# Gated delta rule recurrence: gate loads at a chunk's tail, merged outputs stored by chunk, one step between an inverse's loads and its products

## The chip, the cores and the metric

The kernel runs on 1 core of one Trainium2 chip. The metric is the device time of one execution in microseconds (us). Several executions are timed, and their median stands for the kernel; one more execution is profiled, and its trace is what the rows below come from. Instructions run in order on each of five engines: TensorE (PE), VectorE (DVE), ScalarE (ACT), GpSimd (POOL) and SyncE (SP), which here only issues transfers (DMAs). ACT issues DMAs too. An engine that waits holds up what stands behind it in its own program.

## The reference, cut to what matters

One layer of a streaming encoder for 1024 prompt frames and 8 x 16 sample frames (1152 frames in all), width 1024, in float32:

```
z   = x @ w_in                -> q, k, v of three mixers, gate logits, a, b
o_A = attention over the own chunk and 8 chunks before, with a relative bias
o_B = gated DeltaNet: conv + SiLU, l2-normalised q and k, decay, delta rule, RMSNorm per head
o_C = cross-attention into 256 memory tokens
h   = LayerNorm(alpha * x + (sum_b sigmoid(gate_b) * o_b) @ w_out)
y   = LayerNorm(alpha * h + relu(h @ w_ff1 + b_ff1)^2 @ w_ff2 + b_ff2)
```

The delta rule solves, for each head and each block of frames, a triangular system and then carries a 128 x 128 state from block to block:

```
sol = triangular_solve(I + a_kk, [beta*v | beta*exp(G)*k])    -> u, w
wv  = u - w @ S ;   o = q_dec @ S + a_qk @ wv ;   S = exp(g_end) * S + k_dec^T @ wv
```

The outputs are y, the caches, the last conv inputs and the last states.

## The kernel before, in words

Every product is taken in float32 accuracy: a matrix is split into a high and a low part and three products (high x high, high x low, low x high) are summed. The time falls into four phases: attention (phase_a), cross-attention (phase_c), the delta rule (phase_b) and the output with the feed-forward (phase_out). The change touches phase_b, and through the merged outputs `og` the first part of phase_out.

**Phase_b** works on 8 heads x 3 chunks of 384 frames (three blocks of 128; the third block of chunk 2 holds the samples). It is written as generators that a loop steps one after the other. One turn of the loop is called a round here. In a round, each of these makes one step, to its next `yield`:

- `scans` runs `b_scan`: per block two steps of `b_step`, the sequential recurrence (tile `sc` on PE, `wv` on ACT, the new state `S` on DVE). A chunk's scan starts when its inverse is there and the tails of the chunks up to the second before it are done.
- `tail` runs `b_tail` of the chunk last scanned: for chunk 2 first the sample block (`b_sample`), then RMSNorm (`rst`, `on`), a transpose (`ot`), the product with the gate (`gt`), and `merge`, which adds what `og` already holds (`part`, loaded by SP, added on POOL) and stores the sum to `og` from ACT's queue.
- `invs` runs `b_inverse`: five loads by SP (`at`, `kd`, `bv`, `X`, `Y`), one product of `bv` with beta on DVE, and three levels that double the block size of the inverse, each with products on PE (`t<-X,am`, then `t<-us,Y` and `t<-Y,us`), a copy on ACT (`us`) and two additions on DVE (`X`, `Y`). At the end comes `t<-Y,kbe`, which gives `wT`.
- `mids` prepares the next head (`b_group`: decay factors `E`, products `kk`, `at` written to DRAM; `b_blocks`: the inverses of 16 x 16 blocks, 15 pairs of short DVE instructions `tmp`, `yb`).

After these, `fills` gives independent work: pieces of three matmuls of the remaining gate projections (128x384, tile `ps`), and, once 22 tails are done, of the first half of the output product on the first two chunks (`out_early`, 128x512, tile `ps` too). A round takes 1.35 pieces on average:

```
            if self.inv:
                n += FILL
            else:
                n += FILL0
            for g in streams:
                next(g, None)
            run(mid, 1)
            self.marks.append(self.last)
            run(fill, int(n))
            n -= int(n)
```

What of `fills` is left when the 24th tail is done is run at the end. `order` ties the first matmul of each piece behind the last stream matmul of four rounds before. Within these limits the compiler's scheduler sets the order on each engine: it goes by program order as priority, by its own idea of when each instruction is ready, and by when a buffer comes free. So an instruction can stand earlier in an engine's program than the code has it. Buffers rotate: `X`, `at2`, `gt` and `part` have 2, `Y`, `kd` and `bv` 3. A load whose buffer is still in use waits on SP, and what is queued behind it on SP waits too.

**Phase_out** then loads the rest of `og` (three tiles of 128 frames, `mg`, one buffer), finishes the first half of the output product, does the second half (`op`, with weights `woh`, `wol`), layer norm and the feed-forward.

The names to follow: `b_inverse` at L841 with its loads at L851 to L855 and the product at L856; `b_scan` with the gate load at L904; `b_tail` with `gt` at L930; `merge` with the `part` load at L768, the sum on POOL at L769 and the store at L771; `mg` at L1230.

Of the kernel before, what the change touches and what calls it, by code (L numbers as in the profile page):

```python
# [11 lines left out]
F32 = mybir.dt.float32  # L12
# [7 lines left out]
P = 128  # L20
# [4 lines left out]
NT = SEQ + DB * DT  # L25
CW = 384
NCH = NT // CW
KT = D // P
# [35 lines left out]
class K:  # L64
# [66 lines left out]
    def setup(self):  # L131
        nc, d = self.nc, self.d
        nc.scalar.preload_act_table_set("natural_log_exp_and_others")
        cst = self.const.tile([P, C_END], F32, name="cst")
        self.cst = cst
        self.ident = cst[:, C_ID:C_ID + P]
        self.og = self.dram.tile([KT, P, NT], F32, name="og")
        self.started = set()

        self.gates = [(0, 0), (0, 1), (0, 2), (0, 3), (1, 7)] + [(2, t) for t in range(4)] + [(a, t) for t in range(4, KT) for a in (0, 2)]  # L140
        self.oa, self.oc, self.gb = (self.dram.tile([KT, P, NT], F32, name=n) for n in ("oa", "oc", "gb"))
        self.spq = self.dram.tile([KT, P, NT], F32, name="spq")
        self.spk = self.dram.tile([KT, P, NT], F32, name="spk")
        self.spn = self.dram.tile([2, KT, P, NT], F32, name="spn")
        self.rows = self.dram.tile([2, 8, 9, P], F32, name="rows")
        self.b_dram()
        eps = self.const.tile([P, 4], F32, name="eps")
        nc.vector.memset(eps[:, 0:1], 1e-6)
        nc.vector.memset(eps[:, 1:2], 1e-5)
        nc.vector.memset(eps[:, 2:3], float(np.log(128.0 ** -0.5)))  # L150
        nc.vector.memset(eps[:, 3:4], 1.0)
        self.eps = eps
        self.sums = self.const.tile([P, NT // P, 2], F32, name="sums")
# [608 lines left out]
    def merge(self, t, c, e, pool):  # L762

        nc = self.nc
        dst = self.og[t][:, c * CW:(c + 1) * CW]
        if (t, c) in self.started:
            p = pool.tile([P, CW], F32, name="part", bufs=2)
            nc.sync.dma_start(p, dst)  # L768
            nc.gpsimd.tensor_add(e, e, p)  # L769
        self.started.add((t, c))  # L770
        nc.scalar.dma_start(dst, e)  # L771
# [67 lines left out]
    def b_inverse(self, h, c, pool, ps, res, free):  # L839

        nc, d, B, cst = self.nc, self.d, self.B, self.cst  # L841
        n0 = 3 * c
        npr = 2 if c == 2 else 3
        bank = lambda: ps.tile([P, 512], F32, name="t1", tag="b", bufs=2)
        t3 = lambda name, bufs=2: pool.tile([P, 3, P], F32, name=name, bufs=bufs)
        v = lambda t, m=3: t[:, :m * P].rearrange("p (n t) -> p n t", n=m)
        v3 = lambda t: t.rearrange("p (n t) -> p n t", n=3)
        col = lambda t: t[:, h, n0:n0 + 3].unsqueeze(2).broadcast_to([P, 3, P])
        n = slice(c * CW, (c + 1) * CW)
        X, Y, at, kd, bv = t3("X"), t3("Y", 3), t3("at2"), t3("kd", 3), t3("bv", 3)  # L850
        nc.sync.dma_start(at, self.matrices(self.dat[h % 2], n0, 3))  # L851
        nc.sync.dma_start(kd, v3(self.spn[0][h][:, n]))
        nc.sync.dma_start(bv, v3(self.spn[1][h][:, n]))
        nc.sync.dma_start(X, self.matrices(self.dxy[h % 2][0], n0, 3))
        nc.sync.dma_start(Y, self.matrices(self.dxy[h % 2][1], n0, 3))  # L855
        nc.vector.tensor_mul(bv, bv, col(B["be"]))  # L856
        for l in range(3):
            if l == 2:
                kbe = t3("kbe", 1)
                nc.vector.tensor_mul(kbe, kd, col(B["bg"]))  # L860
                nc.gpsimd.tensor_mul(kd, kd, col(B["kd"]))
            am = t3("am")
            lm = cst[:, C_LV + l * P:C_LV + (l + 1) * P].unsqueeze(1).broadcast_to([P, npr, P])
            nc.gpsimd.tensor_mul(am[:, 0:npr, :], at[:, 0:npr, :], lm)

            m, nb = 16 << l, 4 >> l
            blocks = lambda t, e: t.rearrange("p n (b e m) -> p (n b) e m", e=2, m=m)[:, 0:npr * nb, e, :]
            half = lambda t: t[:, 0:npr * 64].rearrange("p (b m) -> p b m", m=m)
            of = lambda t, n: t[:, n * nb:(n + 1) * nb]
            us = B["us"][l]  # L870
            u, uv, xv, yv = half(bank()), blocks(us, 0), blocks(X, 0), blocks(Y, 1)
            for n in range(npr):
                self.mm(of(u, n), lhsT=am[:, n, :], rhs=of(xv, n), start=True, stop=True)
            nc.scalar.copy(uv, u)
            yield
            if l < 2:
                xp = half(bank())
                for n in range(npr):
                    self.mm(of(xp, n), lhsT=Y[:, n, :], rhs=of(uv, n), start=True, stop=True)
            yp = half(bank())  # L880
            for n in range(npr):
                self.mm(of(yp, n), lhsT=us[:, n, :], rhs=of(yv, n), start=True, stop=True)
            if l < 2:
                nc.vector.tensor_add(xv, xp, xv)
            nc.vector.tensor_add(yv, yp, yv)
            yield
        wt = bank()
        for n in range(3):
            self.mm(wt[:, n * P:(n + 1) * P], lhsT=kbe[:, n, :], rhs=Y[:, n, :], start=True, stop=True)
        while not free():  # L890
            yield
        wT = t3("wT")
        nc.scalar.mul(wT, v(wt), -1.0)
        res[h, c] = Y, bv, wT, kd

    def b_scan(self, h, c, pool, ps, g, r, state, tails):
        nc, d, B = self.nc, self.d, self.B
        aq, qd, eg = g
        Y, bv, wT, kd = r
        n0 = 3 * c  # L900
        samp = c == 2
        npr = 2 if samp else 3
        gate = pool.tile([P, CW], F32, name="gt", bufs=2)
        nc.sync.dma_start(gate, self.gb[h][:, c * CW:(c + 1) * CW])  # L904
        o = ps.tile([P, 512], F32, name="ob", tag="ob", bufs=2)
        for n in range(npr):
            yield from self.b_step(h, n0 + n, n, pool, ps, Y, bv, wT, qd, aq, kd, o, state)
        if samp:
            nc.scalar.dma_start(d["o_ssmp"][h], state[0])
        tails[h, c] = self.b_tail(h, c, pool, ps, o, gate, (Y, bv, wT, qd, aq, kd, o, eg))  # L910

    def b_tail(self, h, c, pool, ps, o, gate, sample):

        nc, d, B = self.nc, self.d, self.B
        n0 = 3 * c
        if c == 2:
            yield from self.b_sample(h, pool, ps, *sample)
        st = pool.tile([P, 4], F32, name="rst", bufs=2)
        on = pool.tile([P, 3, P], F32, name="on", bufs=2)
        for n in range(3):  # L920
            nc.scalar.activation(on[:, n, :], o[:, n * P:(n + 1) * P], AF.Square, accum_out=st[:, n:n + 1])
        nc.vector.scalar_tensor_tensor(st[:, 0:3], st[:, 0:3], 1.0 / P, B["ssq"][:, h, n0:n0 + 3], op0=ALU.mult, op1=ALU.add)
        nc.scalar.activation(st[:, 0:3], st[:, 0:3], AF.Ln)
        nc.scalar.activation(st[:, 0:3], st[:, 0:3], AF.Exp, scale=-0.5)
        nc.vector.tensor_mul(on, o[:, :CW].rearrange("p (n t) -> p n t", n=3), st[:, 0:3].unsqueeze(2).broadcast_to([P, 3, P]))
        yield
        ot = ps.tile([P, 512], F32, name="ot", tag="kk")
        for n in range(3):
            self.transpose(ot[:, n * P:(n + 1) * P], in_=on[:, n, :], identity=self.ident)
        nc.vector.scalar_tensor_tensor(gate, ot[:, :CW], B["ng"], gate, op0=ALU.mult, op1=ALU.mult)  # L930
        self.merge(h, c, gate, pool)
# [262 lines left out]
    def out_early(self, po, pool):  # L1194

        nc, d = self.nc, self.d
# [4 lines left out]
        for c in range(2):  # L1201
            while self.done < 22 + c:
                yield
            n = slice(c * CW, (c + 1) * CW)
            for k in range(KT):
                mg = pool.tile([P, CW], F32, name=("e", "oraw")[k % 2], bufs=2)
                nc.sync.dma_start(mg, self.og[k][:, n])
                hi, lo = self.xh[:, k, n], self.xl[:, k, n]
                nc.scalar.copy(hi, mg)
                nc.vector.tensor_sub(lo, mg, hi.bitcast(F32))  # L1210
            for i in range(3 * c, 3 * c + 3):
# [3 lines left out]
                o = self.psg.tile([P, 512], F32, name="ps", tag="g")  # L1215
                yield from self.out_mm(i, 0, self.w0, o, x)

    def phase_out(self, pool, ps):
        nc, d = self.nc, self.d
# [3 lines left out]
        with self.pool("p2a") as pa:  # L1223
# [3 lines left out]
            for i in range(6, T9):  # L1227
                t = slice(i * P, (i + 1) * P)
                mg = pa.tile([P, KT, P], F32, name="mg", bufs=1)
                nc.sync.dma_start(mg, self.og[:, :, t].rearrange("k p n -> p k n"))  # L1230
                nc.scalar.copy(hh[:, :, t], mg)
                nc.vector.tensor_sub(hl[:, :, t], mg, hh[:, :, t].bitcast(F32))
                nc.sync.dma_start(accs[i], d["x"][i])
# [183 lines left out]
```

## Time and profile before

| what | us |
|---|---|
| median of 3 timed runs | 2750.88 (2748.21 to 2756.87) |
| the profiled execution, timed | 2752.38 |
| its span, first to last instruction | 2750.5 |
| PE busy | 2655.3 (97%) |
| PE weight loads busy | 2464.2 (90%) |
| DVE busy | 1448.3 (53%) |
| ACT busy | 1004.5 (37%) |
| POOL busy | 809.3 (29%) |

The span is 1.9 us shorter than the profiled execution's own time, and that time is 1.5 us above the median. PE's busy time counts a matmul until its modelled end, and matmuls overlap, so 97% doesn't say that PE runs at its peak. Phase_b is the stretch from about 1325 to 1840 us of the span. There PE has gaps, DVE is busiest, and the DMA engines move most.

### The profile page before, as it was taken

The page shows a single profiled execution, that of the slowest core. Times are in us where ns is not written, and L with a number is a line of the kernel's source. Part 1 is how long each engine was busy: PE and PEld are TensorE (multiplying, and loading weights), DVE is VectorE, ACT ScalarE, POOL GpSimd, SP SyncE. Part 2 cuts the span into 40 slices and gives each one's busy share as a digit, 9 for nine tenths or more (in the row PEclk, how much of TensorE's full clock was granted, in tenths as well). Part 3 has the DMA queues.
Part 4 walks back from the last instruction along what each step waited for, and adds up shares of the span by engine and source line. Part 5 has one row for each costly group of instructions (what it writes and reads, how often), then busy time and mean ns, then how long its engine had stood idle before and what let it go on. Part 6 is the DMA issues. An engine that isn't in the chain of part 4 may idle for free.

```text
span 2750.5 us, 45013 instructions
## 1 busy us (share of the span) xinstructions
PE 2655.3 (97%) x16361; PEld 2464.2 (90%) x16361; DVE 1448.3 (53%) x3353; ACT 1004.5 (37%) x2749; POOL 809.3 (29%) x1197
## 2 busy tenths in 40 slices
PE   8999999999999989999989989999999999999997
PEld 7989999999999989888888888878999999999996
DVE  4647484755647563333556666555444444444445
ACT  5646474655647453223433333234211111111113
POOL 2222222222222222212645555323251211211213
PEclk9999999999999999999999999999999999999999
DMA  6343434434343434444866766561210110110101
GB/s 224 104 153 120 163 123 149 148 125 164 114 150 120 163 124 148 164 155 153 252 180 199 211 196 185 175 218 47 79 57 31 54 39 31 54 39 31 61 20 69
DMA packets 263261, 343.27 MB, mean 125 GB/s; under 512 B 55408, under 2 KB 188160, under 8 KB 260480
## 3 DMA queue, kind: packets, MB, share of 16 engines
q1 hardware_dynamic: 201344, 245.93, 28.5%
q10 hardware_dynamic: 61696, 94.47, 10.0%
q8 instruction: 129, 2.11, 0.3%
q14 instruction: 92, 0.75, 0.1%
HBM read 267.69 MB, written 105.13 MB: 136 GB/s over the span
## 4 chain that ended last, share of the span: by engine, by line
PE 81%; DMA 8%; DVE 5%; issue 3%; POOL 2%; ACT 1%; SPq 0%; ACTq 0%; DVEq 0%; POOLq 0%
PE ps L115 48%; PE op L115 16%; PE od L115 3%; PE S L115 3%; PE t L115 2%; PE tb L120 2%; PE sc L115 1%; PE tp L120 1%; PE kk L115 1%; DMA bv<-spn 1%; DVE tmp L786 1%; PE o L115 1%; DMA wraw<-in_w_mem 1%; PE ob L115 1%; DMA kb<-in_cak 1%
## 5 line engine op out<-in xcount | busy, mean ns | idle before, releaser
L115 PE MATMUL ps<-xh,whi 128*128 128x384 f32 x2712 | 950.3, 350 | 10.3 <-POOL whi L168 7.0
L115 PE MATMUL ps<-xh,wlo 128*128 128x384 f32 x2712 | 927.6, 342 | 1.8 <-DVE wlo L169 1.8
L115 PE MATMUL ps<-xl,whi 128*128 128x384 f32 x2712 | 927.3, 342 | 0.0
L115 PEld LDWEIGHTS ps<-xh,whi 128*128 128x128 f32 x2712 | 511.2, 189 | 27.7 <-POOL whi L168 7.0
L115 PEld LDWEIGHTS ps<-xl,whi 128*128 128x128 f32 x2712 | 511.1, 188 | 16.5 <-issue 5.0
L115 PEld LDWEIGHTS ps<-xh,wlo 128*128 128x128 f32 x2712 | 510.2, 188 | 10.0 <-issue 2.5
L1300 DVE TENSOR_TENSOR acc<-op,acc 128x512 f32<-128x512 f32 x252 | 174.0, 691 | 276.2 <-PE op L115 276.1
L168 POOL TENSOR_SCALAR whi<-wraw 128x512 fp32r<-128x512 f32 x261 | 181.4, 695 | 458.2 <-PE ps L115 381.8
L1274 ACT ACTIVATE r<-ps,bf 128x384 f32<-128x384 f32 x96 | 55.6, 581 | 664.7 <-PE ps L115 659.7
L169 DVE TENSOR_TENSOR wlo<-wraw,whi 128x512 fp32r<-128x512 f32 x261 | 194.1, 744 | 163.2 <-POOL whi L168 161.2
L115 PE MATMUL op<-h,uh 128*128 128x512 f32 x576 | 225.6, 392 | 1.2 <-DVE sm L1304 1.2
L115 PE MATMUL op<-h,ul 128*128 128x512 f32 x576 | 226.1, 392 | 0.0
L115 PE MATMUL op<-l,uh 128*128 128x512 f32 x576 | 225.5, 392 | 0.0
L168 POOL TENSOR_SCALAR uh<-r 128x384 fp32r<-128x384 f32 x96 | 55.0, 573 | 491.8 <-ACT r L1275 479.9
L372 POOL TENSOR_SCALAR pt<-pt,sta 128x640 f32<-128x640 f32 (+3 forms) x144 | 111.3, 773 | 278.3 <-DVE sta L371 231.5
L618 DVE SCALAR_TENSOR_TENSOR y<-z,wc,y 128x384 f32<-128x384 f32 (+1 forms) x216 | 132.2, 612 | 28.2 <-ACT y L615 18.3
L115 PEld LDWEIGHTS op<-h,ul 128*128 128x128 f32 x576 | 108.2, 188 | 23.9
L115 PEld LDWEIGHTS op<-h,uh 128*128 128x128 f32 x576 | 108.3, 188 | 19.5 <-DVE sm L1304 2.0
L370 ACT ACTIVATE pt<-pt,sta 128x640 f32<-128x640 f32 (+3 forms) x144 | 101.0, 701 | 64.6 <-DVE sta L369 53.3
L115 PEld LDWEIGHTS op<-l,uh 128*128 128x128 f32 x576 | 108.1, 188 | 15.5
L368 DVE CUSTOM_DVE_ANT_0 pt<-S,tab 128x640 f32<-128x640 f32 (+4 forms) x128 | 83.7, 654 | 52.4 <-PE S L115 38.5
L169 DVE TENSOR_TENSOR ul<-r,uh 128x384 fp32r<-128x384 f32 x96 | 53.6, 560 | 102.0 <-POOL uh L168 102.0
(374 smaller groups left out, 4562.4 us busy)
## 6 DMA issues: line engine op xcount, KB each, us to landing
wraw<-in_w_in SPq DMA_DIRECT2D x160, 256.0 KB
kb<-in_cak SPq DMA_DIRECT2D x16, 1024.0 KB
vb<-in_cav SPq DMA_DIRECT2D x16, 1024.0 KB
wraw<-in_w_ff SPq DMA_DIRECT2D x64, 256.0 KB
w2raw<-in_w_ff SPq DMA_DIRECT2D x64, 256.0 KB
o_aks<-in_cak ACTq DMA_DIRECT2D x32, 496.0 KB
o_avs<-in_cav ACTq DMA_DIRECT2D x32, 496.0 KB
spn<-kn ACTq DMA_DIRECT2D x48, 192.0 KB
```

Source lines behind the costliest of these rows:

```text
L115: ins = self.nc.tensor.matmul(out, **kw)
L120: ins = self.nc.tensor.transpose(out, **kw)
L168: nc.gpsimd.tensor_scalar(hi, raw, 1.0, 0.0, op0=ALU.mult, op1=ALU.add)
L169: nc.vector.tensor_sub(lo, raw, hi.bitcast(F32))
L368: nc.vector.tensor_tensor_reduce(out=P_, in0=S, in1=tab, scale=1.0, scalar=-3e38, op0=ALU.add, op1=ALU.max, accum_out=st[:, 0:1])
L370: nc.scalar.activation(P_, P_, AF.Exp, bias=st[:, 1:2], accum_out=st[:, 2:3])
L372: nc.gpsimd.tensor_scalar(P_, P_, st[:, 3:4], 0.0, op0=ALU.mult, op1=ALU.add)
L618: nc.vector.scalar_tensor_tensor(y[:, :w], z[:, i:i + w], wc[:, i:i + 1], y[:, :w], op0=ALU.mult, op1=ALU.add)
L786: nc.vector.tensor_tensor(tmp[:, 0:t, 0:t], y[:, 0:t, 0:t], m[:, 0:t, t].unsqueeze(1).broadcast_to([72, t, t]), op=ALU.mult)
L1274: nc.scalar.activation(r, p[:, :CW], AF.Relu, bias=bf[:, f:f + 1])
L1300: nc.vector.tensor_add(a, o, a)
```

## The change

Three edits, all around the recurrence:

1. `b_inverse` yields once between its five loads and its first product. So an inverse takes one round more.
2. The gate of a chunk is loaded when its tail begins (`b_tail`), not when its scan begins (`b_scan`).
3. `og` is stored as [tile, chunk, 128, 384], not as [tile, 128, 1152]. A chunk's 128 rows of 1536 bytes lie one behind the other.

```diff
-        self.og = self.dram.tile([KT, P, NT], F32, name="og")
+        self.og = self.dram.tile([KT, NCH, P, CW], F32, name="og")
...
     def merge(self, t, c, e, pool):
-        dst = self.og[t][:, c * CW:(c + 1) * CW]
+        dst = self.og[t, c]
...
     def b_inverse(self, h, c, pool, ps, res, free):
...
         nc.sync.dma_start(X, self.matrices(self.dxy[h % 2][0], n0, 3))
         nc.sync.dma_start(Y, self.matrices(self.dxy[h % 2][1], n0, 3))
+        yield
         nc.vector.tensor_mul(bv, bv, col(B["be"]))
...
     def b_scan(self, h, c, pool, ps, g, r, state, tails):
-        gate = pool.tile([P, CW], F32, name="gt", bufs=2)
-        nc.sync.dma_start(gate, self.gb[h][:, c * CW:(c + 1) * CW])
         o = ps.tile([P, 512], F32, name="ob", tag="ob", bufs=2)
...
-        tails[h, c] = self.b_tail(h, c, pool, ps, o, gate, (Y, bv, wT, qd, aq, kd, o, eg))
+        tails[h, c] = self.b_tail(h, c, pool, ps, o, (Y, bv, wT, qd, aq, kd, o, eg))
...
-    def b_tail(self, h, c, pool, ps, o, gate, sample):
+    def b_tail(self, h, c, pool, ps, o, sample):
         nc, d, B = self.nc, self.d, self.B
         n0 = 3 * c
+        gate = pool.tile([P, CW], F32, name="gt", bufs=2)
+        nc.sync.dma_start(gate, self.gb[h][:, c * CW:(c + 1) * CW])
         if c == 2:
             yield from self.b_sample(h, pool, ps, *sample)
...
     (out_early)
-                nc.sync.dma_start(mg, self.og[k][:, n])
+                nc.sync.dma_start(mg, self.og[k, c])
...
     (phase_out)
-                nc.sync.dma_start(mg, self.og[:, :, t].rearrange("k p n -> p k n"))
+                nc.sync.dma_start(mg, self.og[:, 2, :, (i - 6) * P:(i - 5) * P].rearrange("k p n -> p k n"))
```

**Where the order moves.** Edit 3 alone leaves the order of every engine as it was, and the stores and loads keep their 128 rows of 1536 bytes (`mg`: 512 bytes); only the distance from row to row in DRAM goes from 4608 to 1536 bytes. Edit 2 alone leaves PE, DVE, ACT and POOL as they were and moves the gate load on SP in four of 24 chunks, by two to five places. Edit 1 reorders all engines from the first inverse on. Three places show it; lines after the change are one higher behind L855.

DVE, around the product of `bv` in head 3, chunk 1. Before:

```order
L834 TENSOR_TENSOR qa_17593<-kk,E 128x256
L885 TENSOR_TENSOR Y<-t_17572,Y 128x2x64
L856 TENSOR_TENSOR bv<-bv,be 128x384
L954 SCALAR_TENSOR_TENSOR S_17570<-S_17525,ge,sc 128x128
L860 TENSOR_TENSOR kbe<-kd,bg 128x384
L922 SCALAR_TENSOR_TENSOR rst<-rst,ssq 128x3
L925 TENSOR_TENSOR on<-ob,rst 128x384
L884 TENSOR_TENSOR X<-t_17667,X 128x12x16
```

Now:

```order
L955 SCALAR_TENSOR_TENSOR S_17632<-S_17587,ge,sc 128x128
L886 TENSOR_TENSOR Y<-t_17634,Y 128x2x64
L857 TENSOR_TENSOR bv<-bv,be 128x384
L923 SCALAR_TENSOR_TENSOR rst<-rst,ssq 128x3
L861 TENSOR_TENSOR kbe<-kd,bg 128x384
L169 TENSOR_TENSOR wlo<-wraw,whi 128x512
L926 TENSOR_TENSOR on<-ob,rst 128x384
L885 TENSOR_TENSOR X<-t_17736,X 128x12x16
```

The product of `bv` stands behind the last `Y` of the inverse before in both. One state update, `S`, has gone from behind it to ahead of it.

SP, the loads of the same chunk's inverse. Before:

```order
L904 DMA gt<-gb 128x384
L836 DMA dat_76<-at 128x3x128
L808 DMA kT<-spk 128x384
L810 DMA kq<-spq 128x3x128
L853 DMA bv<-spn 128x384
L854 DMA X<-dxy_79 128x3x128
L855 DMA Y<-dxy_79 128x3x128
```

Now:

```order
L916 DMA gt<-gb 128x384
L809 DMA bb<-rows 128x384
L751 DMA oraw<-oc 128x384
L853 DMA bv<-spn 128x384
L854 DMA X<-dxy_79 128x3x128
L836 DMA dat_76<-at 128x3x128
L852 DMA kd<-spn 128x384
L855 DMA Y<-dxy_79 128x3x128
```

The gate load stands four places ahead of `bv` before and three places now. `X` has followed `bv` in both; `kd` is now one place ahead of `Y`.

PE, behind the last transpose `ot` of phase_b (rows of tile `ps` are pieces of `out_early`, then of phase_out's first half). Before, where the pieces left over end, 96 matmuls behind `ot`:

```order
L115 MATMUL ps<-hi_20707,xh 128x512
L115 MATMUL ps<-lo_20708,xh 128x512
L115 MATMUL ps<-hi_20707,xl 128x512
L115 MATMUL ps<-whi,xh 128x512
L115 MATMUL ps<-wlo,xh 128x512
```

Now, where they end, 29 matmuls behind `ot`:

```order
L115 MATMUL ps<-hi_20503,xh 128x512
L115 MATMUL ps<-lo_20504,xh 128x512
L115 MATMUL ps<-hi_20503,xl 128x512
L115 MATMUL op<-woh,xh 128x512 x3
L115 MATMUL op<-wol,xh 128x512
L115 MATMUL op<-woh,xl 128x512
```

Before, the last three rows of a tile are followed directly by the products that need the first `mg`. Now 67 of the 96 stand ahead of `ot`, between the last steps of the streams, and 18 matmuls of the second half (`op`) stand between the 29 and the products of the first `mg`.

## Rows read from the trace of the kernel before

**Rows 1.** The page, busy time of PE: us, share of the span, instructions.
```profile
PE 2655.3 (97%) x16361; PEld 2464.2 (90%) x16361; DVE 1448.3 (53%) x3353; ACT 1004.5 (37%) x2749; POOL 809.3 (29%) x1197
```

**Rows 2.** Busy time by stretch: length, then each engine, PEclk, DMA share, GB/s.
```profile
0.00:1325.00 1325.00, 1294.50 (x8681) 1229.39 (x8682) 719.90 (x1880) 666.22 (x1838) 330.51 (x634) 0.99 0.44 146
1325.00:1840.00 515.00, 466.31 (x3222) 429.59 (x3222) 310.92 (x842) 170.82 (x606) 258.35 (x306) 0.96 0.68 199
1840.00:2750.00 910.00, 894.49 (x4462) 805.17 (x4460) 417.48 (x631) 167.44 (x305) 220.46 (x257) 0.99 0.15 52
```

**Rows 3.** Waits of DVE, 1325 to 1840: total us, times, longest.
```profile
DVE bv L856 <- DMA bv<-spn: 42.3, 17, 4.9
```

**Rows 4.** DVE's program in time: start, us, in brackets idle before and releaser.
```profile
1413.16 0.90 DVE L856 TENSOR_TENSOR bv<-bv,be 128x384 f32<-128x384 f32 x1 [2.10 <-DMA bv<-spn]
...
1540.53 0.99 DVE L856 TENSOR_TENSOR bv<-bv,be 128x384 f32<-128x384 f32 x1 [3.81 <-DMA bv<-spn]
...
1746.26 0.68 DVE L856 TENSOR_TENSOR bv<-bv,be 128x384 f32<-128x384 f32 x1 [1.52 <-DMA bv<-spn]
1761.52 0.56 DVE L856 TENSOR_TENSOR bv<-bv,be 128x384 f32<-128x384 f32 x1 [4.86 <-DMA bv<-spn]
```

**Rows 5.** PE's program in time, products that waited behind a late `bv`.
```profile
1433.21 0.85 PE L115 MATMUL t<-X,am 128*128 128x64 f32 x6 [0.82 <-DVE X L884]
...
1677.89 1.22 PE L115 MATMUL kk<-we,kd 128*128 128x512 f32 x2 [3.10 <-DVE sb L994]
...
1762.39 0.49 PE L115 MATMUL sc<-bv,Y 128*128 128x128 f32 x2 [2.75 <-DVE S L954]
```

**Rows 6.** Waits of SP's queue, 1325 to 1840: total us, times, longest.
```profile
SPq L904 <- DMA og<-gt: 31.1, 15, 6.1
SPq L852 <- PE kk L115: 26.5, 6, 9.8
```

**Rows 7.** The chain that ended last, 1500 to 1600: start, us, what.
```profile
1531.33 2.95 DMA og<-gt
1536.23 4.27 DMA bv<-spn
...
1574.81 5.97 DMA bv<-spn
```

**Rows 8.** SP's program in time around 1535: start, us, what.
```profile
1532.95 0.34 SPq L751 DMA_DIRECT2D oraw<-oa  x1
1534.30 0.32 SPq L904 DMA_DIRECT2D gt<-gb  x1
...
1536.23 0.63 SPq L853 DMA_DIRECT2D bv<-spn  x1
```

**Rows 9.** The chain that ended last, pace of 72 matmuls of 128x512.
```profile
1845.21 16.95 PE ps L115 x72
```

**Rows 10.** PE's program in time, the last steps of phase_b.
```profile
1809.18 0.55 PE L120 MATMUL ot<-cst,on 128*128 128x128 f32 x3 [0.95 <-DVE on L925]
...
1815.28 0.79 PE L115 MATMUL sc<-bv,Y 128*128 128x128 f32 x2 [0.66 <-DVE S L954]
...
1831.85 0.49 PE L120 MATMUL ot<-cst,on 128*128 128x128 f32 x3
```

**Rows 11.** DVE, ACT and SP in time, from the last `gt` to the first `mg`.
```profile
1836.44 0.62 DVE L930 SCALAR_TENSOR_TENSOR gt<-ot,ng,gt 128x384 f32<-128x384 f32 x1
...
1838.42 0.35 ACTq L771 DMA_DIRECT2D og<-gt  x1
...
1842.73 0.38 SPq L1230 DMA_DIRECT2D mg<-og  x1
...
1846.92 1.04 ACT L1231 CAST xh<-mg 128x1024 fp32r<-128x1024 f32 x1
...
1848.00 1.23 DVE L1232 TENSOR_TENSOR xl<-mg,xh 128x1024 fp32r<-128x1024 f32 x1 [1.63 <-ACT xh L1231]
```

## The prediction

> **What bounds the kernel now.** I read the page's busy times first, then busy time by stretch, then, for the stretch that the change touches, who waited for whom, PE's and DVE's programs in time, SP's queue, and the chain that ended last. PE is busy for 97% of the span [rows 1]. By stretch it is not the same everywhere: from 1325 to 1840 us, the recurrence, PE is busy for 466.3 of 515.0 us, and its clock was granted at 0.96, against 0.99 on either side [rows 2]. So whatever the change is worth must come out of 48.7 us of gaps in this stretch, plus a little of the clock that fell with them, or out of the seam to phase_out behind it.
>
> Where do the gaps come from? On DVE the longest sum of waits that a load ends is one line's: `bv` waits for its load 17 times, 42.3 us in all, at most 4.9 [rows 3]. DVE runs in order, so the state update or the additions behind `bv` are late, and PE waits for them. I went through PE's waits within some 4 us behind such a late `bv`: there are eight, from 1433.21 to 1762.39 us, the longest 3.10 us, 15.6 us together [rows 5]. That is what late loads cost PE directly. The rest of the 42.3 us lies beside other PE work.
>
> Why is `bv` late? SP's queue waited 31.1 us, 15 times, to issue a gate load whose buffer the store `og<-gt` still read, and 26.5 us for `kd`'s buffer [rows 6]. The chain shows what follows: a store of 2.95 us to 1534.28, then the gate load at 1534.30, and `bv` four issues later at 1536.23, landing 4.27 us after that [rows 7, 8]. So edits 1 and 2 aim at real waits.
>
> **The step and the load.** In the code, inverses now take 7 rounds instead of 6, with one more per head for the samples before. I counted the loop's turns from the conditions in the code: 19 per head before, 21 now, 182 in all before and 198 now. How long is a round? The product of `bv` for head 1's first chunk starts at 1413.16, for head 7's at 1746.26 [rows 4]: 333.1 us for six heads, 55.5 us a head, 2.92 us a round.
>
> If the product really came one round behind its load, each of DVE's waits would lose up to 2.92 us. The longest, 4.86 and 3.81 [rows 4], would leave 1.94 and 0.89, and 15.6 us on PE would nearly go. But a program's order counts, not the code's. The order around `bv` shows the product still directly behind the last `Y` of the inverse before, and the load still behind the gate's and the same other loads on SP. The scheduler pulls the product forward to where it thinks the load has landed, in both kernels. I therefore take **0** for this part. Its bounds are -15.6 us, and +26.7 us if all 42.3 us that DVE waits were to show on PE (42.3 - 15.6). I am nearer the middle because the neighbours in both orders are the same, but for one state update.
>
> [...] The row: a load of `bv`, 192 KB, takes 4.27 to 5.97 us [rows 7], more than a round. [...]
>
> **The gate load.** Taken alone, edit 2 moves SP's gate load in four chunks of 24. It stood where its buffer came free, and it stands there still. So SP's 31.1 us [rows 6] stay: **0**. If they went, `bv` would come some 2.1 us earlier in 15 chunks (31.1 / 15), which is the same -15.6 as above and not a second gain. A gate that comes too late for `gt` is excluded for the same reason: it isn't issued later.
>
> **og by chunk.** No order changes, no wait falls away, and rows of 1536 bytes (512 for `mg`) stay. **0**. What a shorter distance between rows does to a transfer no row shows. Transfers of 192 KB took from 2.95 to 5.97 us [rows 7]; that spread, 3 us either way, bounds each of the two that lie one behind the other on the path at the seam, the last store and the first `mg`. The other 60-odd have other work beside them.
>
> **Rounds and pieces.** 16 more rounds draw 1.35 pieces each, so work moves from behind the loop into it. The order shows how much: 67 matmuls of 128x512 that stood behind the last `ot` now stand ahead of it. At 16.95 us for 72 [rows 9], 0.235 us each, that is 15.8 us. PE's work is the same in sum, so this is worth 0 if it only stretches the loop, and -15.8 us if all of it falls into gaps. PE has gaps in 48.7 of 515 us, 9.5% [rows 2], so I take 9.5% of 15.8: **-1.5 us**.
>
> At the loop's end the gain is plainer: the last scan steps ran with hardly any pieces between them, and four waits from 1809.18 to 1815.28 us sum to 3.4 us [rows 10]. Now three to nine piece matmuls stand between these steps: **-3.4 us** (bounds -3.4 and 0).
>
> What covered the seam is then missing. The last `ot` starts at 1831.85 [rows 10]; the last gate product at 1836.44, its store is issued at 1838.42, the first `mg` load at 1842.73, and `mg` is split by 1849.23 (1848.00 + 1.23) [rows 11]. From the gate product that takes 12.8 us, and 17.4 from `ot`. Before, 96 matmuls (22.6 us) lay over it. Now it is 29, and 18 of `op`: 47 x 0.235 = 11.0 us. DVE has only one other row left ahead of the gate product, so I allow 1.3 us from `ot` to it instead of 4.6: 14.1 us against 11.0 leaves PE 3.1 us short, and I add 0.9 for the next weights `woh`, whose loads queue behind `mg`: **+4.0 us**, bounds 0 and 6.4 (17.4 - 11.0).
>
> **Sum.** 0 + 0 + 0 - 1.5 - 3.4 + 4.0 = -0.9 us against the profiled execution's 2752.4: 2751.5. That execution lies 1.5 us above the median of the runs shown, so for a median I forecast 2750 us: no change that can be told. About 0.3%, 8 us, is what a measurement of this kernel can tell from none.
>
> **Rivals.**
>
> *The loads get their step after all.* DVE reaches `bv` later, because the scan's `S` now stands ahead of it, and the 15.6 us on PE go [rows 5]: 2750.9 - 15.6 = 2735 us. For it speaks that two thirds of the inverses wait today [rows 3], and that more pieces between the products give every late result more time; with all 15.8 us of them in gaps it would reach 2720. Against it speak the unchanged neighbours of `bv` on DVE. The Trainium skill, "DMA: Bandwidth & Descriptors", section "Rules for kernel authors", has this rule: issue a transfer early, compute, and wait for it late, and its fixed cost overlaps. By that rule this rival is what happens. The trace agrees in part: 7 of 24 products of `bv` found their load landed.
>
> *A round costs what a round costs, and the kernel is slower.* Scans, tails and inverses step in turn, each tied to others' progress. If the added 16 rounds are latency, not only pieces, each costs up to 2.92 us less its pieces (1.35 x 3 matmuls of 128x384 at three quarters of 0.235, 0.71 us): 2.2 us. At the least it costs PE's gap in a round, 48.7 / 182 = 0.27 us. I take 0.9, a third of the way up, since the streams' own work doesn't multiply: 16 x 0.9 = +14.6 us, 2765 us. For it speaks that the chain of this stretch runs through scan, inverse and their loads and not through pieces alone; against it, that the step added holds no product. It decides from the head's period: two more rounds of pieces take a head from 55.5 to 56.9 us, and above that the change loses. This rival puts it at 58.8.
>
> *The change doesn't do what it says.* That is the forecast: the loads keep their places, and the pieces only move.
>
> **How the numbers follow.** Forecast 0.46, the step that works 0.30, the costly rounds 0.24. These are also the chances of the same, faster and slower. Half of each rival's chance lies beyond its own time, 0.27 in all; from 2732 to 2768 us the range goes 3 us past either one's time, and leaves out some 2 in 10.
>
> **What would show it.** The distance of the two products of `bv` named above: about 342 us with the forecast, 330 or less if the step works, 353 or more if rounds cost. DVE's waits on `bv`, 42.3 us: about as many with the forecast, under 15 if the step works. SP's wait of the gate load on `og<-gt`: still some 30 us. PE idle behind the last `ot`: a wait of 2 to 5 us ahead of the products of the first `mg`. The forecast is wrong if DVE's waits on `bv` fall and PE's gaps with them, or if the head's period passes 57 us by much.

## The result and the profile after

The changed kernel takes 2766.86 us, the median of 9 runs (2760.89 to 2771.80), against 2750.88 us of the kernel before, also of 9 runs. The ratio is 1.0059 (95% interval 1.0046 to 1.0071): some 16 us slower. The execution that was profiled took 2760.89 us, the shortest of the nine, so its trace shows only 8.5 us of the 16 against the one of before (2752.38).

The first row of the page is PE's busy time, as in [rows 1]; under it the row of the stretch from 1325 to 1840 us, which answers to the second line of [rows 2] (here with PE alone: length, PE busy, granted clock, DMA share, GB/s).

```profile
PE 2657.0 (96%) x16361; PEld 2466.5 (89%) x16361; DVE 1440.4 (52%) x3353; ACT 1006.7 (36%) x2749; POOL 808.1 (29%) x1197
```

```profile
1325.00:1840.00 515.00, 461.19 (x3202) 0.95 0.67 196
```

The fixed stretch no longer holds the same work, so I divide both kernels at the last `ot` instead. PE's busy time of the kernel before, up to it and from it to the end:

```profile
1325.00:1831.85 506.85, 459.32 (x3191) 0.96 0.68 198
1831.85:2750.50 918.65, 901.48 (x4492) 0.99 0.16 53
```

And of the changed kernel:

```profile
1325.00:1853.56 528.56, 474.75 (x3257) 0.95 0.66 194
1853.56:2759.10 905.54, 886.62 (x4425) 0.99 0.15 52
```

The last `ot` comes 21.7 us later. 67 matmuls have moved from behind it to ahead of it, and PE's busy time says the same: 15.4 us more ahead, 14.9 less behind. These cancel. What doesn't cancel is idle time (length less busy): 47.5 us became 53.8 ahead of `ot`, 17.2 became 18.9 behind it. 6.3 + 1.7 + 0.6 of busy time are the 8.6 us by which this span is longer. So the loss in this execution is gaps on PE, most of them in the recurrence. What the longer executions lose besides is seen in the run e1 below, the step alone, whose profiled execution took 2772.92 us. Up to its last `ot`:

```profile
1325.00:1864.32 539.32, 479.07 (x3255) 0.94 0.65 190
```

60.3 us idle (12.7 more than before), and 19.8 us more busy time for 64 more matmuls at a clock of 0.94 in place of 0.96.

DVE's and SP's waits of the changed kernel, 1325 to 1870 us (total us, times, longest), to be read beside [rows 3, 6]:

```profile
DVE bv L857 <- DMA bv<-spn: 39.3, 20, 4.5
```

```profile
SPq L851 <- POOL am L865: 36.4, 12, 7.3
SPq L916 <- DMA og<-gt: 29.4, 13, 4.6
SPq L1208 <- DMA og<-gt: 10.3, 2, 9.4
SPq L852 <- PE kk L115: 7.2, 5, 3.6
```

The wait of the load of `at` in the kernel before:

```profile
SPq L851 <- POOL am L864: 10.8, 10, 4.4
```

Edits 1 and 2 did not take away what they aimed at: 39.3 us of waits on `bv` (42.3 before) and 29.4 on the gate's buffer (31.1). What has grown on SP is the wait of the load of `at` for its buffer, from 10.8 to 36.4 us, while that of `kd` on PE's `kk` fell from 26.5 [rows 6] to 7.2. New is one wait of 9.4 us (L1208) ahead of an early load of `og` for the output product. On PE three waits have grown. Before:

```profile
PE sc L115 <- ACT wv L942: 3.9, 5, 2.1
PE t L115 <- DVE Y L885: 3.7, 3, 1.7
PE t L115 <- ACT us L874: 2.1, 4, 0.9
```

After:

```profile
PE t L115 <- DVE Y L886: 12.4, 9, 2.7
PE sc L115 <- ACT wv L943: 7.4, 5, 2.4
PE t L115 <- ACT us L875: 4.2, 6, 2.1
```

The three have grown by 14.3 us in all, PE's gaps ahead of `ot` by 6.3, so others have shrunk. Two of these waits can be followed back to a late `bv`, in DVE's, ACT's and PE's programs (start, us, in brackets idle before and releaser). DVE:

```profile
1448.81 0.56 DVE L857 TENSOR_TENSOR bv<-bv,be 128x384 f32<-128x384 f32 x1 [4.05 <-DMA bv<-spn]
...
1449.89 0.35 DVE L886 TENSOR_TENSOR Y<-t,Y 128x192 f32<-128x192 f32 x1
...
1608.08 0.56 DVE L857 TENSOR_TENSOR bv<-bv,be 128x384 f32<-128x384 f32 x1 [4.15 <-DMA bv<-spn]
...
1609.62 0.15 DVE L923 SCALAR_TENSOR_TENSOR rst<-rst,ssq 128x3 f32<-128x3 f32 x1
```

ACT and PE:

```profile
1609.81 0.20 ACT L924 ACTIVATE rst<-rst 128x3 f32<-128x3 f32 x1 [3.47 <-DVE rst L923]
...
1610.16 0.25 ACT L943 COPY wv<-sc 128x128 f32<-128x128 f32 x1
```

```profile
1450.30 0.94 PE L115 MATMUL t<-Y,kbe 128*128 128x128 f32 x6 [1.41 <-DVE Y L886]
...
1610.46 0.80 PE L115 MATMUL sc<-wv,kd 128*128 128x128 f32 x2 [2.40 <-ACT wv L943]
```

At 1448.81 the product of `bv` has waited 4.05 us; behind it in DVE's program stands the last addition `Y` of another inverse, and PE waits 1.41 us for that. At 1608.08 it has waited 4.15 us; `rst` stands behind it on DVE, the copy of `wv` behind `rst` on ACT, and PE waits 2.40 us for `wv`. In the changed kernel `bv` stands ahead of the last `Y` of another inverse 7 times, in the kernel before twice.

### The profile page after: what moved, and what is told of

It reads as the page before. It is cut to its first block, busy times and chain, and to the rows that moved or that the text cites. A ratio compares the mean times of both kernels' runs of the same rounds, so it can differ in the third digit from the quotient of the medians.

```text
span 2759.1 us, 45012 instructions
## 1 busy us (share of the span) xinstructions
PE 2657.0 (96%) x16361; PEld 2466.5 (89%) x16361; DVE 1440.4 (52%) x3353; ACT 1006.7 (36%) x2749; POOL 808.1 (29%) x1197
## 4 chain that ended last, share of the span: by engine, by line
PE 80%; DMA 9%; DVE 4%; issue 3%; POOL 2%; ACT 1%; SPq 1%; ACTq 0%; DVEq 0%; POOLq 0%
PE ps L115 47%; PE op L115 16%; PE od L115 3%; PE S L115 3%; PE t L115 2%; PE tb L120 2%; DMA bv<-spn 2%; PE tp L120 1%; PE sc L115 1%; PE kk L115 1%; DMA wraw<-in_w_mem 1%; PE o L115 1%; DVE tmp L786 1%; DMA kb<-in_cak 1%; POOL whi L168 1%
## 5 line engine op out<-in xcount | busy, mean ns | idle before, releaser
L115 PEld LDWEIGHTS op<-l,uh 128*128 128x128 f32 x576 | 108.1, 188 | 15.4
```

What stands on the lines that cost most here:

```text
L115: ins = self.nc.tensor.matmul(out, **kw)
```

## The experiments

Each run was timed beside the kernel before on the same chip. "Step" is the yield of edit 1. Ratios are to the kernel before.

| run | edit | median us | ratio (95%) |
|---|---|---|---|
| e1 | edit 1 alone | 2774.10 | 1.0072 (1.0049 to 1.0096) |
| e2 | edits 2 and 3 alone | 2751.51 | 0.9989 (0.9975 to 1.0004) |
| e3 | step ahead of the loads | 2771.46 | 1.0061 (1.0039 to 1.0082) |
| e4 | changed kernel, 1.24 pieces a round | 2749.45 | 0.9984 (0.9967 to 1.0000) |
| e5 | before, 1.47 pieces | 2776.22 | 1.0077 (1.0063 to 1.0091) |
| e6 | changed, 1.30 | 2775.32 | 1.0079 (1.0060 to 1.0097) |
| e7 | before, 1.24 | 2767.35 | 1.0048 (1.0028 to 1.0069) |
| e8 | loads issued in the round before, no step | 2750.75 | 0.9986 (0.9975 to 0.9996) |
| e9 | changed, `bv` tied behind `Y` | 2754.47 | 1.0005 (0.9996 to 1.0014) |
| e10 | changed, `bv` at the third level | 2762.06 | 1.0031 (1.0019 to 1.0043) |
| e11 | no step, `bv` at the third level | 2735.81 | 0.9939 (0.9924 to 0.9955) |
| e12 | changed, 1.26 | 2775.94 | 1.0087 (1.0065 to 1.0109) |
| e13 | changed, third buffer for `at` | 2768.91 | 1.0062 (1.0040 to 1.0083) |
| e14 | no step, `bv` tied behind `Y` | 2733.29 | 0.9941 (0.9921 to 0.9961) |
| e15 | e11, third buffer for the gate | 2739.41 | 0.9948 (0.9930 to 0.9966) |
| e16 | before, 1.36 | 2773.60 | 1.0076 (1.0049 to 1.0103) |
| e17 | e14, 1.36 | 2749.19 | 0.9975 (0.9958 to 0.9993) |
| e18 | e9, 1.24 | 2742.10 | 0.9947 (0.9930 to 0.9965) |

**Which edit.** e1 is the kernel before with the yield, e2 the changed kernel without it, e3 the changed kernel with the yield moved:

```diff
     e3, b_inverse
+        yield
         X, Y, at, kd, bv = t3("X"), t3("Y", 3), t3("at2"), t3("kd", 3), t3("bv", 3)
...
         nc.sync.dma_start(Y, self.matrices(self.dxy[h % 2][1], n0, 3))
-        yield
         nc.vector.tensor_mul(bv, bv, col(B["be"]))
```

> Only the yield between an inverse's loads and its product; the gate load and og as before. Rounds theory (each of the 16 added rounds is latency in the chain of inverses, 1 us a round): 2767 us, ratio 1.006, distance of the fourth and the 22nd product of bv 350 to 358 us against 333. Theory of the split (the loads now come a round earlier than their buffers are free and hold up SP; the wait of the at load on POOL's am is 36.4 us after the change, 10.8 before): 2767 as well, with that wait above 30. Theory that the gate load or the layout of og costs the time: 2751, ratio 1.000.

> Edits 2 and 3 (gate load at the tail, og by chunk) without the yield. Rounds and split theories: 2751 us, ratio 0.998 to 1.002, distance 331 to 336 us. Theory that the gate load or og costs the time: 2763 to 2767.

> The changed kernel with its yield moved ahead of the five loads: the loads and the product are in one round again, as before the change, and the loop still makes 198 rounds. Rounds theory: 2763 to 2771 us (an empty round is as dear wherever it stands), distance 350 to 358. Theory of the split: 2751 (2748 to 2755), the wait of the at load on am back near 11 us.

The step alone costs all of it (1.0072), edits 2 and 3 nothing (0.9989). It costs the same when it stands ahead of the loads and parts nothing (1.0061), so the split of load and product is not the cause. e1 shows one stall whole. Here is SP, then DVE and PE, then PE's busy time in steps of 4 us:

```profile
1480.69 0.44 SPq L810 DMA_DIRECT2D kq<-spq  x1
1485.42 0.32 SPq L809 DMA_DIRECT2D bb<-rows  x1
1485.84 0.38 SPq L853 DMA_DIRECT2D bv<-spn  x1
```

```profile
1490.13 0.56 DVE L857 TENSOR_TENSOR bv<-bv,be 128x384 f32<-128x384 f32 x1 [5.09 <-DMA bv<-spn]
1490.61 0.28 DVE L886 TENSOR_TENSOR Y<-t,Y 128x128 f32<-128x128 f32 x1
```

```profile
1490.94 1.65 PE L115 MATMUL t<-Y,kbe 128*128 128x128 f32 x6 [3.97 <-DVE Y L886]
```

```profile
1484.00:1488.00 4.00, 2.98 (x20) 1.00 0.24 63
1488.00:1492.00 4.00, 1.05 (x5) 0.85 1.04 309
1492.00:1496.00 4.00, 4.00 (x17) 0.50 0.30 78
1496.00:1500.00 4.00, 4.00 (x30) 0.79 0.62 202
```

SP issues nothing from 1481.13 to 1485.42: `bb` stands first in its queue and waits for its buffer, which POOL's `kq` still reads (4.2 us). `bv` behind it is issued at 1485.84 and landed when DVE starts at 1490.13. `Y` stands behind `bv` and PE waits 3.97 us. Then the granted clock goes to 0.50, the 1.2 GHz level: 17 matmuls in 4 us, where the next slice has 30. At 0.50 and 0.79 these two slices lose 2.8 us of work (4 x 0.50 + 4 x 0.21), so a stall of 3.97 us costs 6.8.

**Rounds or pieces.** Only the constant changes:

```diff
-FILL0, FILL = 5, 1.35
+FILL0, FILL = 5, 1.24
```

> The changed kernel with 1.24 pieces a round in place of 1.35, so that 198 rounds draw as many pieces as 182 did (246). Rounds theory: the rounds are latency and lose cover with the pieces; 2763 to 2772 us, distance 340 to 352 of which PE idle grows past 40 us (34.1 in the changed kernel). Theory of the pieces (the added rounds cost only because they draw pieces into a stretch that PE cannot go through any faster, and the pieces are then missing at the seam): 2748 to 2755, distance 331 to 338, idle near 29.

> The kernel before, with 1.47 pieces a round in place of 1.35: 182 rounds, none added, but they draw as many pieces as the changed kernel's 198 did (335 are made in the loop, 24 are left; in the changed kernel 334 and 25; two rounds find no piece to draw, four there). Theory of the pieces (the time goes with the number of pieces drawn into the loop, whatever the rounds): 2763 to 2773 us, ratio 1.004 to 1.008, PE's granted clock from 1324 to 1964 us as low as in the changed kernels. Rounds theory: 2748 to 2755.

> The changed kernel with 1.30 pieces a round (331 made in the loop, 28 left, no round without a piece to draw). Theory of the pieces, by dose: 320 made cost nothing and 334 cost 16 us, so 331 cost 8 to 16: 2758 to 2767 us. Theory of the gap at the end (the gates' pieces run out before 22 tails are done, four rounds draw nothing, and the first load of the output product holds up SP for 9.4 us): 2748 to 2754, as with 1.24, since here none runs out.

> The kernel before, with 1.24 pieces a round: 300 made in the loop, 59 left behind it. Theory of the pieces: fewer in the loop are better or the same, 2740 to 2751 us. Theory that 182 rounds with 1.35 and 198 with 1.24 do well because some 320 pieces are what the streams need as cover: more gaps in the loop, 2757 to 2770 us.

198 rounds with 1.24 pieces cost nothing (0.9984; the fourth and the 22nd product of `bv` are 336.6 us apart, against 362.1 in e1), so an added round is not dear by itself. 182 rounds with 1.47 pieces, none added, are as slow as the change (1.0077), which looked like the pieces. But 1.30 is no better than 1.35, and fewer pieces on the kernel before are slower too (1.0048): neither goes by dose. Two numbers close to the ones that cost nothing tell more:

> The changed kernel with 1.26 pieces a round (324 made in the loop, 35 left; with 1.24 320 and 39). bv stands ahead of the last Y in 4 inverses (2 with 1.24, 6 with 1.30, 7 with 1.35). Order theory: 2752 to 2760 us. Theory of the pieces: 2751 to 2757. If any other order than the two of 2750 us is simply slower by chance: 2765 to 2776.

> The kernel before with 1.36 pieces a round in place of 1.35: 320 pieces are made in the loop (318 before; 320 in the changed kernel with 1.24), the order of every engine changes from the first pieces on. Theory of the pieces' number: 2748 to 2756 us. Chance (1.35 is one order out of many, and most others are slower): 2760 to 2776.

1.26 where 1.24 was free costs 24 us (0.0087 x 2752), and 1.36 where 1.35 was free costs 21, with 320 pieces, as many as e4 drew. So neither the number of rounds nor that of pieces sets the time by itself: at 320 to 324 pieces both prices occur. What is left for these two runs is the order that the scheduler makes. PE's busy time up to the last `ot` and behind it, e4:

```profile
1325.00:1829.98 504.98, 451.63 (x3199) 0.97 0.70 201
1829.98:2748.90 918.92, 902.76 (x4491) 0.99 0.16 52
```

e16:

```profile
1325.00:1854.30 529.30, 475.53 (x3214) 0.93 0.66 192
1854.30:2773.10 918.80, 901.46 (x4492) 0.99 0.16 53
```

Behind `ot` both need what the kernel before needs, 918.65 us. Ahead of it e16 has 53.8 us idle (47.5 before), and 16.2 us more busy time for 23 more matmuls, at most 5.4 us of work at 0.235 us [rows 9]: the other 10.8 us or more go with a clock of 0.93 in place of 0.96. e4 has gaps as long (53.4 us), but its clock was 0.97, and it needs 7.7 us less busy time than the kernel before. Gaps and the clock together make an order dear.

Pieces are not cleared by this. All eight runs whose loop makes 331 to 335 pieces (the change, e1, e3, e5, e6, e13, and e9 and e10 below) are 0.6 to 0.9% slower than their like with 318. So many pieces may be dear by themselves, and other orders (e7, e12, e16) dear for other reasons; no run parts the two. The wait on SP that the second theory for e6 names is still there in e6 (8.9 us), so that run doesn't test it. But in the changed kernel it falls into the loop's end, where PE is idle for 2.1 us in 33.6 up to the last `ot`, so it can't be what costs 16:

```profile
1820.00:1853.56 33.56, 31.48 (x181) 1.00 0.31 102
```

**Loads a round earlier without a round more.** e8 splits the five loads off into a function that the inverse before calls ahead of its last yield, and again in each round in which it waits for its turn:

```diff
             nc.vector.tensor_add(yv, yp, yv)
+            if l == 2:
+                ahead()
             yield
```

> Edits 2 and 3, no added round, but the five loads of the next inverse are issued in the last round of the one before (23 of 24 inverses), so that load and product are a round apart in the code with 182 rounds and the same pieces as before. If late loads of bv are worth what PE waits behind them (15.6 us in the kernel before): 2732 to 2745 us, ratio 0.993 to 0.998, DVE's wait on bv under 20 us. If the scheduler only moves them back, or the buffers aren't free any earlier: 2748 to 2755, that wait still 33 to 42 us.

```profile
DVE bv L873 <- DMA bv<-spn: 40.1, 18, 5.1
```

0.9986, which is no more than e2, and DVE's waits on `bv` stayed at 40.1 us. An earlier load in the code does not part load and product in the order. From the issue of the load to the start of its product it took 4.5 us on average in the kernel before, 4.1 in the changed kernel and 4.3 in e8 (means over the fourth to the 24th product).

**DVE's waits on bv.** e9 and e14 tie the product's place; e10 and e11 move it to the third level of its own inverse and tie it behind the second `Y` there:

```diff
     e9, e14
-        nc.vector.tensor_mul(bv, bv, col(B["be"]))
+        mul = nc.vector.tensor_mul(bv, bv, col(B["be"]))
+        if B.get("ly") is not None:
+            dep = mybir.DependencyInfo(mybir.DependencyClass.NoSync, mybir.DependencyReason.DATA)
+            self.tc.add_manual_dep(mul.ins, B["ly"], dep, reason="behind Y")
...
-            nc.vector.tensor_add(yv, yp, yv)
+            add = nc.vector.tensor_add(yv, yp, yv)
+            B["ly"] = add.ins.name
```

> The changed kernel with one tie of order added on DVE: the product of bv stands behind the last addition Y of the inverse before. In the changed kernel it stands ahead of it in 7 inverses (2 in the kernel before), waits for its load there 12.5 us, and the last products of that inverse on PE wait behind it. Order theory (this is what the added step costs: about 8 us more gaps on PE and the clock that falls with them): 2750 to 2758 us, PE's wait of t on DVE's Y down from 12.4 us to under 6. Theory of the pieces (334 pieces drawn into the loop cost by themselves): 2762 to 2772, whatever the order on DVE.

> The changed kernel with the product of bv moved to the third level of its own inverse and tied behind the second Y addition there, so that its load has some 10 us more and DVE shouldn't wait for it at all. Order theory: 2735 to 2755 us, since no addition stands behind a wait for bv any more. Theory of the pieces: 2758 to 2770; DVE's waits on bv vanish (under 5 us), but the loop is as long as the pieces make it.

> Edits 2 and 3, no added round, and the product of bv at the third level as in the run above. If DVE's 42 us of waits on bv are worth what PE waits behind them (15.6 us in the kernel before) and the clock besides: 2730 to 2743 us, ratio 0.991 to 0.996. If the streams are held elsewhere (the loads of kd, X and Y, the gate's store): 2746 to 2753.

> Edits 2 and 3 without the added round, with the tie of the run e9 (the product of bv behind the last Y addition of the inverse before). Order theory (the tie undoes what the step did): no gain here, 2748 to 2754 us. Additive theory (DVE's 40 us of waits on bv cost 13 to 16 us in either kernel, the step costs its 16 us elsewhere): 2733 to 2741.

The tie returned the changed kernel to 1.0005, as the order theory had it. But e14 shows that this was no undoing: without the step the tie gains as much (0.9941), and so does e11 (0.9939). The theory that `bv` ahead of `Y` is what the step costs fell; waits on `bv` cost about 0.5% in either kernel, and the step costs its 0.6% (e14 to e9) or 0.9% (e11 to e10) without them too. e16 speaks against it as well: there `bv` stands ahead of another inverse's last `Y` once, and the run is as slow as the change. Where the waits went, e9's DVE, then e14's DVE and SP show:

```profile
DVE bv L857 <- DMA bv<-spn: 0.5, 1, 0.5
```

```profile
DVE bv L856 <- DMA bv<-spn: 0.6, 1, 0.6
```

```profile
1459.91 0.34 DVE L888 TENSOR_TENSOR Y<-t,Y 128x192 f32<-128x192 f32 x1
1460.18 0.54 DVE L856 TENSOR_TENSOR bv<-bv,be 128x384 f32<-128x384 f32 x1
...
1476.70 0.60 DVE L856 TENSOR_TENSOR bv<-bv,be 128x384 f32<-128x384 f32 x1
```

```profile
1460.10 0.32 SPq L853 DMA_DIRECT2D bv<-spn  x1
```

A load issued at 1460.10 can't be for the product at 1460.18; it is for the one at 1476.70, 16.6 us later. On average 17.8 us lie between load and product here, where 4.5 did before: the load comes no earlier in the code, the product comes later. Nobody needed the product early: in the changed kernel the fourth one, of head 1's first chunk, is made at 1407.26, and the last `Y` of its own inverse, without which its first reader `sc<-bv,Y` can't start, comes at 1449.89 (in the rows of the result).

PE's busy time up to the last `ot`, e9 and then e14:

```profile
1325.00:1846.20 521.20, 472.95 (x3264) 0.96 0.68 197
```

```profile
1325.00:1813.00 488.00, 449.96 (x3186) 0.97 0.71 206
```

With the waits gone in both, the step still means 48.3 us idle against 38.0, and 23.0 us more busy time for 78 more matmuls (at most 18.3 us of work).

**Buffers.** One number each:

```diff
     e13
-        X, Y, at, kd, bv = t3("X"), t3("Y", 3), t3("at2"), t3("kd", 3), t3("bv", 3)
+        X, Y, at, kd, bv = t3("X"), t3("Y", 3), t3("at2", 3), t3("kd", 3), t3("bv", 3)
...
     e15
-        gate = pool.tile([P, CW], F32, name="gt", bufs=2)
+        gate = pool.tile([P, CW], F32, name="gt", bufs=3)
```

> The changed kernel with a third buffer for at (the tile at2), so that SP doesn't hold the loads behind it for a buffer that POOL's am still reads (36.4 us, 12 times, in the changed kernel; 10.8 before). PE's order stays as it is but for a few rows. Theory of SP's queue (the added round makes SP reach the load of at before its buffer is free, and all loads behind it come late): 2748 to 2757 us, that wait under 8 us. If that wait lies beside others: 2763 to 2771, and SP waits elsewhere.

> The run e11 (no step, the product of bv at the third level) with a third buffer for the gate tile gt, so that SP needn't hold its load for the store og<-gt (32.0 us in e11). If that wait still keeps loads from the streams: 2722 to 2732 us. If it is covered by now: 2733 to 2739.

```profile
SPq L851 <- POOL am L865: 32.9, 11, 7.5
```

e13 is inconclusive: the time did not fall (1.0062), but the wait hardly did either, to 32.9 us. So what the wait for `at` costs stays untested. It is 32.9 to 37.2 us in the slow runs with the step and 21.4 and 16.0 in the two at 1.24 that are not slow (e4, e18); but e5, e7 and e16, slow without the step, have 8.7 to 14.1. e15 took the gate's wait only from 32.0 to 24.3 us and gained nothing (0.9948 against 0.9939).

**Other orders without the waits.**

> The run e14 (no added round, the tie that takes DVE's waits on bv away; 2733 us) with 1.36 pieces a round. With the waits on bv in place 1.36 cost 21 us against 1.35. If late loads of bv are what makes one order dearer than another: 2729 to 2739 us. If the order at 1.35 is a lucky one for other reasons too: 2746 to 2758.

> The run e9 (the changed kernel with the tie; 2754 us) with 1.24 pieces a round, the number that brought the changed kernel to 2749 without the tie. If the tie's 13 to 18 us add to any order: 2730 to 2738 us. If 2749 was that order's luck and the tie makes another order: 2742 to 2756.

Neither theory holds cleanly. 1.36 costs 0.3% with the tie (0.9975 against 0.9941) where it cost 0.8% without it: the order still matters, but less. At 1.24 the tie gains 0.4% (0.9947 against 0.9984). In four orders out of four it gained, 0.4 to 1.0% (at 1.36 the run without the tie, e16, also lacks edits 2 and 3). And the step is free twice where the constant keeps the pieces at 320: 0.9984 against 0.9989 (e4, e2), and with the tie 0.9947 against 0.9941 (e18, e14).

## Why the prediction was wrong

The forecast was 2750 us and no change; the change costs 16. The time lies inside the range, 1 us below its upper end, and close to the second rival's 2765.

**The step and the load (0, bounds -15.6 and +26.7): this term failed.** The step measured by itself is +20 us (e1: 0.0072 x 2754), inside the bounds. The argument was right in its first half: the loads keep their places and the product is pulled forward (4.1 us from load to product, 4.5 before), so the waits stay (39.3 us, against 42.3). It was wrong to go on from there to 0. I let the step cost or gain something through `bv` alone, and took the neighbours of `bv` at one place, head 3's second chunk, for a sign that little had moved, while edit 1 had reordered every engine. The runs show the price elsewhere: with the waits on `bv` gone the step costs 0.6 to 0.9%, as with them (0.7%, e2 against the change), and e9 has 10.2 us more idle time on PE ahead of the last `ot` than e14. Where the pieces are held at 320 it costs nothing (e4, e18), and with four pieces more it costs 24 us (e12). So what the step costs comes with the pieces that it draws into the loop or with the order that they make, not with the load; which of the two it is, and by which wait, stays open.

**The rival of the costly rounds hit the number and not the cause.** Its sign was seen: from the fourth to the 22nd product of `bv` it takes 353.8 us (1407.26 to 1761.06), where 353 or more stood for it. But 198 rounds without extra pieces cost nothing (e4), and 182 rounds lose as much by one hundredth of a piece a round (e16). That the number came close is luck.

```profile
1407.26 0.76 DVE L857 TENSOR_TENSOR bv<-bv,be 128x384 f32<-128x384 f32 x1 [1.25 <-DMA bv<-spn]
...
1761.06 0.56 DVE L857 TENSOR_TENSOR bv<-bv,be 128x384 f32<-128x384 f32 x1 [2.82 <-DMA bv<-spn]
```

**The gate load (0) and og by chunk (0): right.** e2 has both and is at 0.9989; SP's wait is 29.4 us.

**Pieces (-1.5): no such gain.** The moved matmuls came at full price, 15.4 us of busy time ahead of `ot` and 14.9 less behind, and the gaps ahead of `ot` grew by 6.3 us where I had let them shrink. I had given this term no upward bound; the eight runs with 331 pieces or more suggest that it needed one.

**Loop end (-3.4): right.** From the last `ot` but one on, the four waits of [rows 10] are gone, and one is left, on PE:

```profile
1838.00 0.49 PE L115 MATMUL ob<-wv,qa 128*128 128x128 f32 x2 [0.15 <-ACT wv L980]
```

What grew lies ahead of that.

**The seam (+4.0): 2.7 us, but not where I put it.** From the last `ot` to the end the changed kernel needs 905.54 us, 13.1 less than before, where 67 x 0.235 = 15.8 us of work had gone. The path to the first `mg`, beside [rows 10, 11], on PE and on DVE:

```profile
1853.56 0.49 PE L120 MATMUL ot<-cst,on 128*128 128x128 f32 x3
...
1865.70 0.50 PE L115 MATMUL ps<-whi,xl 128*128 128x512 f32 x1 [0.37 <-DVE xl L1233]
...
1946.07 0.63 PE L120 MATMUL tp<-cst,acc 128*128 128x128 f32 x4 [1.50 <-DVE xl L1254]
```

```profile
1854.14 0.62 DVE L931 SCALAR_TENSOR_TENSOR gt<-ot,ng,gt 128x384 f32<-128x384 f32 x1 [4.10 <-issue]
...
1864.42 1.23 DVE L1233 TENSOR_TENSOR xl<-mg,xh 128x1024 fp32r<-128x1024 f32 x1 [2.93 <-ACT xh L1232]
```

From `ot` to the split `mg` it takes 12.1 us (1864.42 + 1.23 - 1853.56), not 14.1, and the 47 matmuls cover it but for 0.37 us. The wait of 2 to 5 us that I had named there did not come. A later wait, 1.50 us ahead of the transposes `tp`, is one of those that make up the rest.

**The step that works (rival, 2735 us)** did not come about by the change. What it priced did: with the waits on `bv` taken away otherwise, the kernel without the step takes 2733 us (e14). The rule that I had cited for it, to issue a transfer early and wait for it late (the Trainium skill, "DMA: Bandwidth & Descriptors", section "Rules for kernel authors"), agrees with e14: there the wait on `bv` is 0.6 us. The late half of it was what was missing here (e8, with the early half alone, gained nothing over e2).

What stays open is why the order at 1.35 with 182 rounds and the one at 1.24 with 198 are good. Of ten other orders without the tie, nine were slower by 0.5 to 0.9% (the change, e1, e3, e5, e6, e7, e12, e13, e16) and one, e8, which differs least from that of before, was not. No single wait was shown to make up the difference.

## What to carry to other kernels

Where a scheduler sets the order, an edit that adds a step changes every engine's order, and here a hundredth or two in the constant beside it, which does that too, cost 21 to 24 us of 2750: move such a constant a little before you credit or blame the edit. Before loads are issued earlier, look whether the first reader of what waits for them needs it yet; to move the product late gained 13 to 15 us here at 1.35, to move its load early nothing. The version to keep is e14 or e11, with edits 2 and 3, without the step and with the product late: 0.994 of the kernel before.

## What was not expected of the hardware

A single wait of PE can be followed by a low clock that costs most of as much again: 3.97 us idle to 1490.94 in e1, then 2.8 us of work lost at 0.50 and 0.79. In e16 at least 10.8 of the 22.5 us by which the last `ot` came later are busy time at the lower clock, and 6.2 are gaps. And a third buffer for `at` hardly shortened SP's wait for it (36.4 to 32.9 us).
